# Feed-forward of latents and context: twelve of 22 pairs of up tiles as seven block products, two weight sums by accumulating transfers

## The chip, the core and the metric

The kernel runs on one core of one Trainium2 chip. The metric is device time in microseconds (us); lower is better. One run gives 1257.7 us as the median of three (1257.22 to 1257.75).

## What is computed

A gated-linear-attention block with its feed-forward, then a second block of two layers over 256 latent tokens and 256 context tokens, width 1024, all in float32. The change lies in the feed-forward of the second block's first layer, which both token sets pass through:

```python
def swiglu_ffn(h, w_in, w_out):
    a, g = jnp.split(h @ w_in, 2, axis=-1)
    return (jax.nn.silu(a) * g) @ w_out
# second_block, layer i:
    h = h + g2_l * swiglu_ffn(ada_norm(h, norm_ffn[i], sh2_l, sc2_l), ffn_w_in[i], ffn_w_out[i])
    if ctx_out:      # true for layer 0 only
        hc = hc + g2_c * swiglu_ffn(ada_norm(hc, norm_ffn[i], sh2_c, sc2_c), ffn_w_in[i], ffn_w_out[i])
```

`ffn_w_in` is 1024 x 5632 (the `a` half, then the gate half), `ffn_w_out` 2816 x 1024.

## The kernel before, in words

**Float32 as three products.** Every large matrix product is done in the type fp32r. Each operand is held as a rounded part `h` and a remainder `l`, and `mm3` (L192 to L195) issues three matmuls: h·h, l·h, h·l. Activations are split when they are made, weights when they arrive.

**Weights as a stream.** All weights stand in memory as units of 128 x 1024 floats (512 KB), in the order of use (`UNITS`). `w_load` (L147) brings a unit into one of five `raw` buffers through the SP queue; `w_split` (L161) writes its `wh` on ACT (L178, a cast) and its `wl` on DVE (L179, a subtraction) into two of twelve `w` buffers. `wnext` hands the next unit to the code and asks for loads and splits a few units ahead (`cap`, 3).

**The feed-forward of layer 0.** The hidden width 2816 is 22 feature tiles of 128. For a feature tile f there is a *pair of up tiles*: one unit for `a`, one for the gate, each 8 blocks of 128 x 128 over the input width. `ffn_up` (L1122) multiplies each of the pair's units with the 512 tokens of `fT` (latents and context side by side): 2 units x 8 blocks x 3 matmuls, each with 512 columns, so 48 matmuls. `ffn_act` (L1109) applies Silu on ACT, multiplies on DVE and splits the result. The first two pairs are done by `ffn_up_first` (L1132), context first, in matmuls of 256 columns.

The 22 pairs run in two parts of 11. After each part `ffn_down0` (L1149) multiplies the part's features with `ffn_w_out`, for each half of the output columns: in the first part for all four token tiles at once, in the second for the two context tiles and then for the two latent tiles. `gated` (L1078) scales the sum and adds it to the residual, two DVE instructions for each token tile and half. In the last half of the latents, `to_T` (transposes on PE, L232) for the context of the next layer is called after the third weight unit.

**Other work in the same stretch.** `ada_jobs` streams the modulation weights: 512 KB for a step into one of two `a` buffers (L304), then one or two DVE reductions of 128 x 1024 (L324). `ada_run` advances it at fixed places of the code: two steps after each pair, one after each unit of `ffn_down0`.

**Order.** Except in stretches marked as ordered by hand, the order of instructions on each engine is laid down when the program is built. A planner takes, for each engine, instructions whose operands its own time estimates call ready, the earlier in the code the sooner. On the chip each engine then runs its list strictly in order: one that waits for an operand holds all behind it. On the GpSimd (POOL) queue, as on SP's, the same holds for transfers.

**PSUM.** Eight banks of 128 x 512 floats. A regular pair uses two; `ffn_down0` with four tiles uses four. An engine that reads a bank and a matmul that writes the same bank follow each other in the code's order, even where they touch different columns.

## Time and profile before

| | |
|---|---|
| time, median of 3 runs | 1257.7 us |
| the profiled execution's own time | 1256.72 us |
| its span, first to last instruction | 1254.9 us |
| granted TensorE clock | 0.999 |
| PE busy | 1244.0 us (99%) |
| DVE busy | 919.9 us (73%) |
| ACT busy | 688.2 us (55%) |
| POOL busy | 78.7 us (6%) |
| the feed-forward of layer 0 | from about 565 to 944 us of the span |

The profiled execution is 1 us under the median. A matmul's listed duration includes its passage through the array, so consecutive matmuls overlap in the list; what one costs is read from the distance between starts. The same holds in a smaller measure for DVE and ACT.

### The profile page before, as it was taken

Reading aid. Unit: us, or ns where it says so; the run is one execution under the profiler, and the core shown is the slowest. Engines: PE = TensorE matmul, PEld = TensorE weight load, DVE = VectorE, ACT = ScalarE, POOL = GpSimd, SP = SyncE. Lnnn points to the kernel's source line nnn. Section 1 sums busy time; section 2 is a strip of 40 time slices with the busy share of each in tenths; the row PEclk is TensorE's granted clock in tenths of the full one; section 3 lists DMA queues with packets and bytes.
Section 4 is the critical chain, followed back from the end, with each engine's and each line's share of the span. In section 5 each row is a group of like instructions: output and inputs, shape, how many; then the busy total and the mean of one; then the engine's idle time right before and its main releaser. Section 6 shows DMA issues by size and latency. Waiting matters only on the chain.

```text
span 1254.9 us, 18667 instructions
## 1 busy us (share of the span) xinstructions
PE 1244.0 (99%) x6872; PEld 1043.2 (83%) x6872; DVE 919.9 (73%) x1638; ACT 688.2 (55%) x1344; POOL 78.7 (6%) x137
## 2 busy tenths in 40 slices
PE   9999999999999999999999999999999999999997
PEld 8888889898888777789888888887888777999997
DVE  6959888697989887777877767633667988655555
ACT  8575655666549888655232222323456897544443
POOL 1010000030100000001000000000003220000000
PEclk9999999999999999999999999999999999999999
DMA  8647687787673333463656877633662324656650
GB/s 304 189 151 237 192 289 268 271 277 246 198 249 111 105 110 118 160 197 118 213 177 206 259 266 249 205 100 102 197 204 76 113 84 131 219 187 185 186 185 34
DMA packets 68507, 231.22 MB, mean 184 GB/s; under 512 B 8048, under 2 KB 8736, under 8 KB 68416
## 3 DMA queue, kind: packets, MB, share of 16 engines
q1 hardware_dynamic: 68128, 229.68, 57.0%
q8 instruction: 54, 0.88, 0.3%
q10 hardware_dynamic: 288, 0.35, 0.1%
q14 instruction: 37, 0.30, 0.1%
HBM read 228.93 MB, written 1.07 MB: 183 GB/s over the span
## 4 chain that ended last, share of the span: by engine, by line
PE 95%; ACT 2%; DVE 1%; issue 1%; DMA 0%; POOL 0%; SPq 0%; POOLq 0%; ACTq 0%
PE b L193 28%; PE b L194 28%; PE b L195 28%; PE b L1000 2%; PE b L1469 1%; PE b L981 1%; PE b L232 1%; PE b L1455 1%; PE b L562 1%; PE b L962 1%; PE b L963 1%; PE b L951 1%; PE b L1436 1%; DVE wl L179 0%; DMA t<-in_xt_dram 0%
## 5 line engine op out<-in xcount | busy, mean ns | idle before, releaser
L178 ACT CAST wh<-raw 128x1024 fp32r<-128x1024 f32 (+1 forms) x308 | 320.7, 1045 | 392.8 <-PE b L194 292.4
L179 DVE TENSOR_TENSOR wl<-raw,wh 128x1024 fp32r<-128x1024 f32 (+1 forms) x308 | 372.5, 1216 | 154.9 <-ACT wh L178 151.9
L193 PE MATMUL b<-t,wh 128*128 128x256 f32 (+1 forms) x1120 | 365.7, 327 | 0.0
L194 PE MATMUL b<-t,wl 128*128 128x256 f32 (+1 forms) x1120 | 365.6, 327 | 0.0
L195 PE MATMUL b<-t,wh 128*128 128x256 f32 (+1 forms) x1120 | 365.3, 327 | 0.0
L193 PE MATMUL b<-wh,t 128*128 128x512 f32 (+1 forms) x748 | 299.2, 402 | 1.2 <-ACT t L250 0.6
L194 PE MATMUL b<-wh,t 128*128 128x512 f32 (+1 forms) x748 | 294.8, 394 | 0.0
L195 PE MATMUL b<-wl,t 128*128 128x512 f32 (+1 forms) x748 | 294.7, 394 | 0.0
L193 PEld LDWEIGHTS b<-t,wh 128*128 128x128 f32 x1120 | 210.7, 188 | 22.2
L194 PEld LDWEIGHTS b<-t,wl 128*128 128x128 f32 x1120 | 210.8, 188 | 21.9
L195 PEld LDWEIGHTS b<-t,wh 128*128 128x128 f32 x1120 | 210.5, 188 | 20.4 <-DVE t L251 0.2
L195 PEld LDWEIGHTS b<-wl,t 128*128 128x128 f32 x748 | 140.4, 188 | 34.2
L193 PEld LDWEIGHTS b<-wh,t 128*128 128x128 f32 x748 | 140.4, 188 | 32.2 <-ACT t L250 1.0
L194 PEld LDWEIGHTS b<-wh,t 128*128 128x128 f32 x748 | 140.8, 188 | 30.1 <-DVE t L251 0.5
L324 DVE CUSTOM_DVE_ANT_0 a<-a,crow 128x1024 f32<-128x1024 f32 x96 | 117.6, 1233 | 28.8 <-DMA a<-in_ada_dram 28.3
L324 DVE CUSTOM_DVE_ANT_0 t<-a,crow 128x1024 bf16<-128x1024 f32 x64 | 78.5, 1237 | 7.3 <-DMA a<-in_ada_dram 7.1
L1112 DVE TENSOR_TENSOR t<-b,t 128x512 f32<-128x512 f32 (+1 forms) x42 | 23.7, 564 | 59.4 <-PE b L195 52.2
L205 POOL TENSOR_TENSOR c<-c,mhalf 128x1 f32<-128x1 f32 x21 | 14.2, 676 | 539.0 <-DVE c L204 538.9
L339 POOL TENSOR_TENSOR mod<-mod,bcol 128x8 f32<-128x8 f32 x20 | 13.4, 671 | 475.1 <-DVE mod L324 472.7
L1118 ACT CAST t<-t 128x512 fp32r<-128x512 f32 (+1 forms) x42 | 21.7, 516 | 28.6 <-DVE t L1112 28.6
L212 ACT ACTIVATE t<-t 128x512 f32<-128x512 f32 x40 | 24.8, 624 | 10.8 <-DVE t L1081 6.4
L1445 ACT ACTIVATE t<-b,c,c 128x512 f32<-128x512 f32 x32 | 26.0, 812 | 3.5 <-POOL c L1443 3.5
(244 smaller groups left out, 1212.6 us busy)
## 6 DMA issues: line engine op xcount, KB each, us to landing
raw<-in_wst_dram SPq DMA_DIRECT2D x310, 512.0 KB, 4.4
a<-in_ada_dram SPq DMA_DIRECT2D x96, 512.0 KB, 4.4
t<-in_rpb_dram SPq DMA_DIRECT2D x16, 256.0 KB, 4.5
t<-row SPq DMA_DIRECT2D x12, 256.0 KB, 5.1
t<-in_ctx_dram SPq DMA_DIRECT2D x8, 256.0 KB, 5.6
t<-in_xt_dram SPq DMA_DIRECT2D x4, 256.0 KB, 5.8
t<-in_x_dram SPq DMA_DIRECT2D x4, 256.0 KB, 6.5
crow<-in_cvec_dram SPq DMA_DIRECT2D x2, 512.0 KB
```

Of the source, the lines that this page charges most:

```text
L178: A.copy(out=h[:, :n], in_=raw[:, :n])
L179: V.tensor_tensor(out=l[:, :n], in0=raw[:, :n], in1=h[:, :n], op=ALU.subtract)
L193: T.matmul(o, lhsT=lh, rhs=rh, start=first, stop=False)
L194: T.matmul(o, lhsT=ll, rhs=rh, start=False, stop=False)
L195: T.matmul(o, lhsT=lh, rhs=rl, start=False, stop=last)
L205: G.tensor_tensor(out=ms[:, 3:4], in0=ms[:, 2:3], in1=mhalf[:, 0:1], op=ALU.pow)
L212: A.activation(out=junk[hf], in_=halves[hf], func=AF.Square, scale=1.0 / 32.0, accum_out=ms[:, hf:hf + 1])
L324: V.tensor_tensor_reduce(out=raw if ci == n_c - 1 else t2([D], BF16), in0=raw, in1=crow[ci], scale=1.0, scalar=0.0, op0=ALU.mult, op1=ALU.add,
L1000: T.matmul(po[e * 64:(e + 1) * 64, cols_], lhsT=v, rhs=probs[(head, "l" if lat_q else "c")][:, c, :], start=(c == 0), stop=(c == n_c - 1))
L1112: V.tensor_tensor(out=a, in0=pg_[:, :n], in1=a, op=ALU.mult)
L1118: A.copy(out=h, in_=a)
L1445: A.activation(out=pl, in_=sl, func=AF.Exp, scale=r, bias=mx[:, 1:2], accum_out=mx[:, 2:3])
```

## The change

For feature tiles 10 to 21 the pair of up tiles is done as a 2 x 2 by 2 x 2 block product in seven block products in place of eight. The blocks of the weights are `a` and gate, each by the lower and upper 512 of the input width; the blocks of the data are latents and context, by the same halves. Each block product is 4 blocks x 3 matmuls of 256 columns.

- `ffn_up7` issues the seven products. Four of them (the first, third, fifth and seventh) accumulate one after the other in the same bank `r`, which is copied out between them: the third continues the sum that the first left, and so on. The second and fourth go to the two halves of bank `r23`, the sixth to `r4`. In all 84 matmuls of 256 columns, three ACT copies, two Silus, seven DVE operations of 256 columns, and the split of the result.
- The four sums of weight blocks are made for each pair as it arrives. `w_load` takes a third `raw` buffer `z`: half a unit of `a` is loaded into it by SP, and two transfers from the POOL queue add a half of the gate unit onto `z` and the other half of the gate unit onto the gate's own buffer. `pair_sums`, a generator with four steps, does the other two sums on DVE and the splits: three of 1024 columns, one of 512. The steps are called from within the pair before (`run(conv, 2)` at its start, one each after its second and fourth product).
- The four sums of data blocks are made once, by `token_sums`, during the second half of the first `ffn_down0`. For them `to_T` keeps the unsplit transposed data in `fX`.
- The latents and the context stand in separate tiles `fL` and `fC`, so that regular pairs (`ffn_up`) issue 96 matmuls of 256 columns in place of 48 of 512.
- Three parts of 8, 8 and 6 pairs replace two of 11. `ada_run` is not called in the seven-product pairs, and twice for each unit of `ffn_down0` with four tiles. `load_gates(0, 5)` is called after each part. The last `to_T` is called after the second unit.

```diff
@@ -26,7 +26,8 @@
 NFT = FH // P
-HALF = NFT // 2
+PARTS = ((0, 8), (8, 16), (16, 22))
+F_SEVEN = 10
@@ -58,11 +59,11 @@
     u += o + o
-    for part in range(2):
-        for f in range(part * HALF, (part + 1) * HALF):
+    for lo, hi in PARTS:
+        for f in range(lo, hi):
             u += [("f", "ffn_in0", P * f), ("f", "ffn_in0", FH + P * f)]
-        dn = [("h", "ffn_out0", part * HALF + f, 512 * h) for h in range(2) for f in range(0, HALF, 2)]
-        u += dn if part == 0 else dn + dn
+        dn = [("h", "ffn_out0", f, 512 * h) for h in range(2) for f in range(lo, hi, 2)]
+        u += dn if hi < NFT else dn + dn
     kv = [("h", "gqa_qkv", 2 * k, D) for k in range(4)]
@@ -149,6 +150,14 @@
             raws[wpos[0]] = raw
+            if seven(UNITS[wpos[0]]) and UNITS[wpos[0]][2] >= FH:
+                x, y = [wst[SLOT[UNITS[wpos[0] + n]]] for n in (-1, 0)]
+                z = sb.tile([P, 1024], F32, tag="raw", bufs=5, name=nm("raw"))
+                nc.sync.dma_start(out=z[:, 0:512], in_=x[:, 0:512])
+                G.dma_start(out=z[:, 0:512], in_=y[:, 0:512], accum_op=ALU.add)
+                G.dma_start(out=raw[:, 0:512], in_=y[:, 512:1024], accum_op=ALU.add)
+                raws[wpos[0]] = (raw, z)
             wpos[0] += 1
@@ -162,7 +171,7 @@
             raw = raws.pop(i)
-            n = 512 if UNITS[i][0] == "h" and UNITS[i][1] == "ffn_out0" and (UNITS[i][2] % HALF) == HALF - 1 else 1024
+            n = 1024
             h = sb.tile([P, 1024], F32R, tag="w", bufs=NW, name=nm("wh"))
@@ -178,21 +187,25 @@
+    def seven(u):
+        return u[1] == "ffn_in0" and u[2] % FH >= P * F_SEVEN
     def wnext(kind):
         w_split(i + 1)
-        while wpos[1] < len(UNITS) and wpos[1] - wpos[2] + 1 < cap[0]:
+        while wpos[1] < len(UNITS) and wpos[1] - wpos[2] + 1 < cap[0] and not seven(UNITS[wpos[1]]):
             w_load(wpos[1] + 4)
-    def mm3(o, lh, ll, rh, rl, first, last):
-        T.matmul(o, lhsT=lh, rhs=rh, start=first, stop=False)
-        T.matmul(o, lhsT=ll, rhs=rh, start=False, stop=False)
-        T.matmul(o, lhsT=lh, rhs=rl, start=False, stop=last)
+    def mm3(o, lh, ll, rh, rl, first, last, onto=False):
+        T.matmul(o, lhsT=lh, rhs=rh, start=first, stop=False, skip_group_check=onto)
+        T.matmul(o, lhsT=ll, rhs=rh, start=False, stop=False, skip_group_check=onto)
+        T.matmul(o, lhsT=lh, rhs=rl, start=False, stop=last, skip_group_check=onto)
@@ -223,7 +236,7 @@
-    def to_T_steps(xns, dst, t0, scale=None, bias=None):
+    def to_T_steps(xns, dst, t0, scale=None, bias=None, keep=None):
@@ -240,7 +253,7 @@
             else:
-                r = t2([n])
+                r = t2([n]) if keep is None else keep[k]
                 if k % 2:
@@ -1098,11 +1111,12 @@
-    fT = new_T2()
+    fL, fC = new_T(), new_T()
+    fX = [t2([2, S]) for _ in range(KD)]
     o_half(1, 2, hc, 1)
     o_half(0, 0, lat, 0)
-    o_half(1, 0, lat, 0, lambda: to_T(xn, fT, S, mod(0, 1, 4), mod(0, 1, 3)))
+    o_half(1, 0, lat, 0, lambda: to_T(xn, fC, 0, mod(0, 1, 4), mod(0, 1, 3), [z[:, 1, :] for z in fX]))
     xn = [normed(t) for t in lat]
@@ -1119,43 +1133,152 @@
-    def ffn_up(L, src, n):
+    def ffn_up(L, src, n, conv=iter(())):
         ps_ = []
             o = bank()
-            for k in range(KD):
-                mm_f(o[:, :n], u, src, k, 0, n, k == 0, k == KD - 1)
+            for t, X in enumerate(src):
+                for k in range(KD):
+                    mm_f(o[:, t * S:(t + 1) * S], u, X, k, 0, S, k == 0, k == KD - 1)
+            run(conv, 2)
             ps_.append(o)
-    def ffn_up_first(src):
+    def ffn_up_first():
             for k in range(KD):
-                mm_f(os_[-1][:, S:N2], us[-1], src, k, S, S, k == 0, k == KD - 1)
-        to_T(xn, src, 0, mod(0, 0, 4), mod(0, 0, 3))
+                mm_f(os_[-1][:, S:N2], us[-1], fC, k, 0, S, k == 0, k == KD - 1)
+        to_T(xn, fL, 0, mod(0, 0, 4), mod(0, 0, 3), [z[:, 0, :] for z in fX])
         z = []
             for k in range(KD):
-                mm_f(os_[n][:, 0:S], us[n], src, k, 0, S, k == 0, k == KD - 1)
+                mm_f(os_[n][:, 0:S], us[n], fL, k, 0, S, k == 0, k == KD - 1)
             if n % 2:
-    def ffn_down0(hf, uu, tiles, between=None):
+    sT = {}
+    def token_sums(j):
+        lo, hi, q = fX[j], fX[j + KD // 2], t2([2, S])
+        V.tensor_tensor(out=q[:, 1, :], in0=hi[:, 1, :], in1=lo[:, 1, :], op=ALU.subtract)
+        V.scalar_tensor_tensor(out=q[:, 0, :], in0=q[:, 1, :], scalar=-1.0, in1=lo[:, 0, :], op0=ALU.mult,
+                               op1=ALU.subtract)
+        V.tensor_tensor(out=lo[:, 1, :], in0=lo[:, 0, :], in1=lo[:, 1, :], op=ALU.subtract)
+        V.scalar_tensor_tensor(out=lo[:, 0, :], in0=q[:, 0, :], scalar=-1.0, in1=hi[:, 0, :], op0=ALU.mult,
+                               op1=ALU.subtract)
+        for z, names in ((q, (2, 1)), (lo, (4, 3))):
+            h, l = t2([2, S], F32R), t2([2, S], F32R)
+            A.copy(out=h, in_=z)
+            V.tensor_tensor(out=l, in0=z, in1=h, op=ALU.subtract)
+            for i, name in enumerate(names):
+                sT[(name, j)] = (h[:, i, :], l[:, i, :])
+    def pair_sums(f, got):
+        i = wpos[1]
+        assert UNITS[i] == ("f", "ffn_in0", P * f)
+        w_load(i + 4)
+        x, (y, z) = raws.pop(i), raws.pop(i + 1)
+        wpos[1] += 2
+        a, b = slice(0, 512), slice(512, 1024)
+        def parts(r):
+            h = sb.tile([P, 1024], F32R, tag="w", bufs=NW, name=nm("wh"))
+            l = sb.tile([P, 1024], F32R, tag="w", bufs=NW, name=nm("wl"))
+            A.copy(out=h, in_=r)
+            V.tensor_tensor(out=l, in0=r, in1=h, op=ALU.subtract)
+            got.append((h, l))
+        parts(x)
+        yield
+        V.tensor_tensor(out=z[:, b], in0=z[:, a], in1=y[:, b], op=ALU.add)
+        parts(z)
+        yield
+        parts(y)
+        yield
+        V.tensor_tensor(out=x[:, a], in0=z[:, b], in1=x[:, b], op=ALU.add)
+        hl = sb.tile([P, 1024], F32R, tag="w", bufs=NW, name=nm("w"))
+        A.copy(out=hl[:, a], in_=x[:, a])
+        V.tensor_tensor(out=hl[:, b], in0=x[:, a], in1=hl[:, a], op=ALU.subtract)
+        got.append((hl[:, a], hl[:, b]))
+        yield
+    def splits(n):
+        for _ in range(n):
+            w_split(wpos[1] + 1)
+            yield
+    def ffn_up7(got, conv):
+        wpos[2] += 2
+        r, r23, r4 = bank(), bank(), bank()
+        c1, c2 = t2([2, S]), t2([2, S])
+        H = KD // 2
+        def prod(o, n, c, X, first=True):
+            h, l = got[n]
+            for j in range(H):
+                k = slice(c + j * P, c + (j + 1) * P)
+                mm3(o, h[:, k], l[:, k], *X(j), first and j == 0, j == H - 1, not first)
+        run(conv, 2)
+        prod(r[:, 0:S], 0, 0, lambda j: fL[j])
+        A.copy(out=c1[:, 0, :], in_=r[:, 0:S])
+        prod(r23[:, 0:S], 0, 512, lambda j: fL[H + j])
+        got[0] = None
+        V.tensor_tensor(out=c1[:, 0, :], in0=r23[:, 0:S], in1=c1[:, 0, :], op=ALU.add)
+        run(conv)
+        prod(r[:, 0:S], 1, 512, lambda j: sT[(2, j)], False)
+        A.copy(out=c1[:, 1, :], in_=r[:, 0:S])
+        A.activation(out=c1[:, 0, :], in_=c1[:, 0, :], func=AF.Silu)
+        prod(r23[:, S:N2], 2, 512, lambda j: sT[(4, j)])
+        run(conv)
+        prod(r[:, 0:S], 1, 0, lambda j: sT[(1, j)], False)
+        got[1] = None
+        A.copy(out=c2[:, 0, :], in_=r[:, 0:S])
+        V.tensor_tensor(out=c2[:, 1, :], in0=c1[:, 1, :], in1=c2[:, 0, :], op=ALU.subtract)
+        V.tensor_tensor(out=c2[:, 0, :], in0=r23[:, S:N2], in1=c2[:, 0, :], op=ALU.add)
+        V.tensor_tensor(out=c2[:, 0, :], in0=c2[:, 0, :], in1=c1[:, 0, :], op=ALU.mult)
+        prod(r4[:, 0:S], 3, 0, lambda j: fC[H + j])
+        V.tensor_tensor(out=c2[:, 1, :], in0=r4[:, 0:S], in1=c2[:, 1, :], op=ALU.add)
+        prod(r[:, 0:S], 2, 0, lambda j: sT[(3, j)], False)
+        V.tensor_tensor(out=c2[:, 1, :], in0=r[:, 0:S], in1=c2[:, 1, :], op=ALU.add)
+        A.activation(out=c2[:, 1, :], in_=c2[:, 1, :], func=AF.Silu)
+        V.tensor_tensor(out=c2[:, 1, :], in0=r[:, 0:S], in1=c2[:, 1, :], op=ALU.mult)
+        a = c2.rearrange("p t s -> p (t s)")
+        h, l = t2([N2], F32R), t2([N2], F32R)
+        A.activation(out=h, in_=a, func=AF.Copy, scale=-1.0)
+        V.scalar_tensor_tensor(out=l, in0=a, scalar=-1.0, in1=h, op0=ALU.mult, op1=ALU.subtract)
+        return h, l
+    def ffn_down0(hf, uu, tiles, between=None, conv=None):
         ac = {t: bank() for t in tiles}
-        for f2 in range(0, HALF, 2):
+        for f2 in range(0, len(uu), 2):
             u = wnext(("h", "ffn_out0"))
-            for j in range(min(2, HALF - f2)):
+            for j in range(2):
                 f = f2 + j
                 for t in tiles:
-                    mm_h(ac[t], u, j, uu[f], t, f == 0, f == HALF - 1)
-            ada_run(adaC)
-            if f2 == 4 and between is not None:
+                    mm_h(ac[t], u, j, uu[f], t, f == 0, f == len(uu) - 1)
+            ada_run(adaC, 2 if len(tiles) == 4 else 1)
+            if hf == 1 and len(sT) < 16:
+                token_sums(f2 // 2)
+            if conv is not None and f2 >= len(uu) - 4:
+                run(conv, 2)
+            if f2 == 2 and between is not None:
                 between()
@@ -1178,18 +1301,29 @@
-    for part in range(2):
+    got = []
+    for lo, hi in PARTS:
         uu = []
-        for f in range(HALF):
-            if part == 0 and f < 2:
-                uu += ffn_up_first(fT) if f == 0 else []
+        for f in range(lo, hi):
+            nxt = []
+            if f + 1 < hi:
+                conv = pair_sums(f + 1, nxt) if f + 1 >= F_SEVEN else iter(())
             else:
-                uu.append(ffn_up(0, fT, N2))
-            ada_run(adaC, 2)
-        if part == 0:
-            load_gates(0, 5)
-            for hf in range(2):
-                ffn_down0(hf, uu, (2, 3, 0, 1))
+                conv = splits(2) if f >= F_SEVEN else iter(())
+            if f < 2:
+                uu += ffn_up_first() if f == 0 else []
+            elif f < F_SEVEN:
+                uu.append(ffn_up(0, (fL, fC), N2, conv))
+            else:
+                uu.append(ffn_up7(got, conv))
+            got = nxt
+            if f < F_SEVEN:
+                ada_run(adaC, 2)
+        load_gates(0, 5)
+        if hi < NFT:
+            ffn_down0(0, uu, (2, 3, 0, 1))
+            got = []
+            ffn_down0(1, uu, (2, 3, 0, 1), None, pair_sums(hi, got) if hi >= F_SEVEN else None)
         else:
@@ -1646,8 +1780,7 @@
             k, c = s[2], s[3]
-            n = 1 if s[1] == "ffn_out0" and k % HALF == HALF - 1 else 2
-            a[i].reshape(P, 2, 512)[:, :n] = m[k * P:(k + n) * P, c:c + 512].reshape(n, P, 512).transpose(1, 0, 2)
+            a[i].reshape(P, 2, 512)[...] = m[k * P:(k + 2) * P, c:c + 512].reshape(2, P, 512).transpose(1, 0, 2)
     return a
```

More of the change, by code (lines that the diff above doesn't have):

```diff
@@ L1524, in net @@
     tok_T(toks[0], 0, ups)
-    up2 = ffn_up(1, eT, S)
+    up2 = ffn_up(1, (eT,), S)
     tok_T(toks[1], 1, ups)
```

2 lines of the change are left out of this document (1 added, 1 removed).

## The prediction

> **What bounds the kernel now.** I read the page's busy times and its chain first, then a table by stretches of the feed-forward (columns: stretch, its us, busy us and instructions of each engine, granted clock, DMA share, GB/s).
>
> ```profile
> span 1254.9 us, 18667 instructions
> PE 1244.0 (99%) x6872; PEld 1043.2 (83%) x6872; DVE 919.9 (73%) x1638; ACT 688.2 (55%) x1344; POOL 78.7 (6%) x137
> PE 95%; ACT 2%; DVE 1%; issue 1%; DMA 0%; POOL 0%; SPq 0%; POOLq 0%; ACTq 0%
> ...
> 565.00:690.00 125.00, 125.00 (x610) 103.61 (x609) 96.18 (x148) 42.42 (x65) 6.92 (x18) 1.00 0.57 179
> 690.00:752.00 62.00, 62.00 (x268) 49.86 (x267) 44.16 (x68) 12.51 (x13) 1.52 (x3) 1.00 0.80 261
> 752.00:875.00 123.00, 123.00 (x527) 98.84 (x526) 64.24 (x85) 35.15 (x46) 3.35 (x3) 1.00 0.52 166
> ```
>
> PE is busy through all of the first part's pairs (565 to 690), its down products (690 to 752) and the second part's pairs (752 to 875), at clock 1.00. So a matmul taken out here shortens the kernel, as long as nothing new makes PE wait. What a matmul costs is read from starts: the first and last of 66 consecutive matmuls of 512 columns, then of 38 consecutive ones of 256 columns, from the next layer's up products.
>
> ```profile
> 584.74 0.39 PE L194 MATMUL b<-t,wl 128*128 128x512 f32 x1
> ...
> 599.97 0.40 PE L193 MATMUL b<-t,wh 128*128 128x512 f32 x1
> ...
> 1099.76 0.28 PE L194 MATMUL b<-t,wl 128*128 128x256 f32 x1
> ...
> 1104.10 0.28 PE L195 MATMUL b<-t,wh 128*128 128x256 f32 x1
> ```
>
> 15.23/65 = 0.2343 us, and 4.34/37 = 0.1173 us: half the columns cost half the time. The weight load in front of each does not show.
>
> **The change part by part. PE first.** A regular pair is 48 x 0.2343 = 11.25 us. A seven-product pair is 84 x 0.1173 = 9.85 us. Twelve pairs save 12 x 1.39 = 16.7 us. The regular pairs 2 to 9 go to 96 x 0.1173 = 11.26 us: 8 x 0.01 = +0.1 us. The down products keep their count.
>
> The Trainium skill, "TensorE: Matmul & The Clock Gate", section "Back-to-back issue gap", gives a sustained spacing of 81 ns at 128 columns and 131 ns at 512, which would make a narrow matmul dear for its columns. The rows above differ from it in both size and ratio, and the measurement decides.
>
> **What must stay hidden beside PE: DVE and ACT in a seven-product pair.** Their cost too is read from starts. The DVE rows (from two stretches) and the ACT rows:
>
> ```profile
> 600.40 1.22 DVE L179 TENSOR_TENSOR wl<-raw,wh 128x1024 fp32r<-128x1024 f32 x1
> 601.54 1.22 DVE L324 CUSTOM_DVE_ANT_0 a<-a,crow 128x1024 f32<-128x1024 f32 x1
> ...
> 607.85 0.69 DVE L1119 TENSOR_TENSOR t<-t,t 128x512 fp32r<-128x512 f32 x1
> 608.45 1.22 DVE L324 CUSTOM_DVE_ANT_0 t<-a,crow 128x1024 bf16<-128x1024 f32 x1
> ...
> 250.32 0.43 DVE L808 TENSOR_TENSOR t<-t,t 128x256 fp32r<-128x256 f32 x1
> 250.67 1.22 DVE L324 CUSTOM_DVE_ANT_0 t<-a,crow 128x1024 bf16<-128x1024 f32 x1
> ...
> 578.11 1.04 ACT L178 CAST wh<-raw 128x1024 fp32r<-128x1024 f32 x1
> 579.05 0.62 ACT L1118 CAST t<-t 128x512 fp32r<-128x512 f32 x1
> ...
> L1462 ACT COPY t<-b x64: 359/388/513, 985.4 to 1052.4; 128x256 f32<-128x256 f32 x64
> L1111 ACT ACTIVATE t<-b 128x256 f32<-128x256 f32 x20 | 7.6, 379 | 1.6 <-PE b L195 1.6
> ```
>
> DVE takes 1.14 us for 1024 columns, 0.60 for 512, 0.35 for 256. For a pair: three subtractions of 1024 (3.42), two sums, the remainder of the fourth and that of the result, all of 512 (4 x 0.60 = 2.40), and seven operations of 256 (2.45): 8.3 us of 9.85, or 84%. ACT: three casts of 1024 (0.94 each by starts), two of 512 (0.62), three copies and two Silus of 256 (0.39 and 0.38): 6.0 us, 60%. Both fit, if in time.
>
> **The handovers.** Here is what the change adds to PE's path. The third product writes the bank `r` that ACT must first copy; so do the fifth and seventh; the fourth writes bank `r23`, which DVE reads after the second. At each only one product of 12 x 0.1173 = 1.41 us lies between, so from the start of the last matmul before to the first matmul behind there is 1.41 + 0.12 = 1.53 us. How soon a reader follows:
>
> ```profile
> 616.60 0.39 PE L195 MATMUL b<-t,wh 128*128 128x512 f32 x1
> ...
> 617.10 0.69 DVE L1112 TENSOR_TENSOR t<-b,t 128x512 f32<-128x512 f32 x1 [2.47 <-PE b L195]
> ```
>
> 0.50 us after that start, DVE is there. With 0.4 us for its own work, some 0.6 us of slack remains. An instruction that is under way can take it. One of DVE's 1.14 us, met at random, has more than 0.6 left in 47% of cases, 0.27 too much on average: at 84% busy 0.84 x 0.47 x 0.27 = 0.11 us. A second one queued ahead adds 1.14; I let that happen in a quarter of the cases, 0.29. On ACT, 0.60 x 0.36 x 0.17 = 0.04 us at each of three. Together 0.5 us for a pair, an estimate from these rows. The ends are 0 (every handover free) and 4 x 1.7 = 6.8 (every one behind two long instructions); the value lies near the low end because three of the four handovers are ACT's. 12 x 0.5 = +6.0 us.
>
> **The adding transfers.** No transfer from POOL's queue stands in this trace. The nearest rows are SP's:
>
> ```profile
> raw<-in_wst_dram SPq DMA_DIRECT2D x7, 512.0 KB, 3.7
> ...
> t<-in_rpb_dram SPq DMA_DIRECT2D x16, 256.0 KB, 4.5
> ...
> out_dram<-t SPq DMA_DIRECT2D x3, 256.0 KB, 2.0
> ...
> t<-in_gk_up_dram SPq DMA_DIRECT2D x2, 32.0 KB, 6.6
> ```
>
> So a load of 256 KB is 2.0 to 4.5 us, an adding one 2.0 to 6.6 behind it (not under 2.0, as it too moves 256 KB and reads its target besides). `z` needs both in turn: 4.0 to 11.1 us; I take 8. The buffer for the `z` of pair n+2 is that of pair n+1's gate unit, free once it is split, and that waits for two `w` buffers (of twelve, seven hold pair n's parts), free after pair n's second product: 2.8 + 0.94 + 1.14, so about 5 us into pair n. `z` is there 3 us into pair n+1 (1 us before its start to 6 us into it). PE needs its parts at the third product of pair n+2, another 9 us on, so the transfers' length costs nothing by itself. What a late one can do is hold DVE's list at the sum on `z` with the urgent bank readers behind it: that is the main rival. Extra bytes: 1.75 MB for a pair in 9.85 us, 178 GB/s, under the 261 of the second stretch.
>
> **The rest, all beside PE.** One part more is eight `gated` more, 16 x 0.60 = 9.6 us of DVE, while the next pair uses the four banks that are free. `token_sums` makes DVE's time for a down unit 1.14 + 2 x 1.2 + 2.6 = 6.1 us against PE's 24 x 0.2343 = 5.6, 2 us over four units; splits made ahead cover it, since ACT's splits stood 122.3 us waiting for PE to free `w` buffers. The waits between 565 and 860 us, the `a` reductions after 722 us, and the end of the last context down product:
>
> ```profile
> ACT wh L178 <- PE b L194: 122.3, 34, 5.0
> ...
> DVE a L324 <- DMA a<-in_ada_dram: 28.3, 19, 4.0
> ...
> L324 DVE CUSTOM_DVE_ANT_0 a<-a,crow x26: 1218/1225/1227, 722.1 to 802.2; 128x1024 f32<-128x1024 f32 x26
> ...
> 900.32 0.69 DVE L1080 TENSOR_TENSOR t<-b,t 128x512 f32<-128x512 f32 x1 [1.42 <-PE b L195]
> ...
> 908.01 0.88 DVE L219 TENSOR_SCALAR t<-t,c 128x512 f32<-128x512 f32 x2 [0.66 <-POOL c L205]
> ...
> 924.62 1.69 PE L232 MATMUL b<-cm,t 128*128 128x128 f32 x14
> ```
>
> Eight weight units fewer take 8 loads off SP. Eight more 256 KB gate rows (`load_gates`) go on it; they are needed a down product later. The last context norm has less time: it was done 8.6 us after the context's last product (900.3 to 908.9), and PE came to the transposes at 924.6. Now it comes to them after 36 + 24 matmuls of 0.2343, 14 us, still behind the norm. Nothing for any of these; if the last cover fails, 1 to 3 us.
>
> **Sum.** -16.7 + 0.1 + 6.0 = -10.6 us: span 1254.9 to 1244.3, that execution 1256.7 to 1246.1. The median is 1.0 above the profiled execution: 1257.7 - 10.6 = 1247.1 us.
>
> **Rivals.** *Full saving*: every handover meets its 0.6 us. For it: list order lets bank readers come early. 1257.7 - 16.6 = 1241.1.
>
> *Late sums (slower)*: the list order is laid down with estimated transfer times, and DVE stands at the sum on `z` while the second product's reader queues behind. For it: DVE already waited 19 times, 28.3 us in all, up to 4.0 us, for `a` transfers. Against it: no wait for a `raw` load is among the long ones of that stretch. Ten pairs are exposed (each part's first is loaded long before). A lateness of L costs (L - 0.6) x 10: at the mean 1.5 us, 9 us, still faster; it decides from 2.3 us on; at 4.0 us, 34 - 16.6 = +17, so 1275. The Trainium skill speaks for this one: "SBUF — State Buffer", section "A bandwidth-pool intuition that's wrong (but worth ruling out)", has a POOL-issued transfer wait for its descriptors behind a DVE copy, 620 ns becoming about 3100; the same page exempts DVE's two-input operations, which fill these pairs, and no run here shows either. With those 2.5 us as L the formula would give +2 us, an estimate.
>
> *DVE full (no change)*: the 26 `a` reductions that ran from 722 to 802 us, far ahead of the place where the code has them, are pulled into the first seven-product pairs, which have 1.5 us free each, and so each handover meets a full engine. Against it: at most six or seven pairs are hit. PE loses the saved 1.39 us in each: 1256 to 1258.
>
> *Narrow matmuls dearer*: the seven products change nothing if 256 columns cost more than 11.25/84 = 0.134 us. The 38 matmuls above stand against it. By the skill's two spacings, interpolated to 98 ns, the ratio would be 0.75 for half the columns: 12 x 3.4 + 8 x 5.5 = +85 us, 1343.
>
> **How the numbers follow.** Forecast (1243 to 1252) 0.47; full saving 0.22; DVE full 0.10; late sums beyond 2.3 us 0.19; narrow matmuls 0.02. About 0.2% (2.5 us) is what a measurement of this kernel can tell from no change. Faster is the first two: 0.69; same 0.10; slower 0.21. The range runs from the full saving, 1240.5, to late sums of about 2.7 us, 1262, and leaves out the longer ones and the last rival, some 0.15 together.
>
> **What would show it.** Right: 256-column starts 0.117 us apart in the seven-product pairs, a pair in 9.9 to 10.6 us, PE's idle time there under 12 us, released by ACT copies or the DVE sum of `r23`. Wrong: DVE idle at the sum on `z` with POOL's transfer as releaser; a pair at 11 us or more; DVE over 95% busy in the first six.

## The result and the profile after

The changed kernel takes 1311.9 us (1308.8 to 1319.2) against 1257.7 us: ratio 1.044, 95% interval 1.040 to 1.048. It is 54 us slower, where 10.6 us less was forecast.

The page of the changed kernel, the lines that answer to those shown of before (span, busy times, the chain by engine), with the clock in 40 slices (9 is 90% or more); the last line is the clock of before:

```profile
span 1309.4 us, 20652 instructions
PE 1256.4 (96%) x7688; PEld 1091.3 (83%) x7688; DVE 989.6 (76%) x1790; ACT 718.5 (55%) x1416; POOL 100.5 (8%) x161
...
PEclk9999999999999999999999788998999999999999
...
PE 28%; DMA 3%; DVE 3%; ACT 2%; issue 1%; POOL 0%; POOLq 0%; ACTq 0%; DVEq 0%; SPq 0%
...
PEclk9999999999999999999999999999999999999999
```

The feed-forward by stretches (stretch, its us, busy us and instructions of PE, PEld, DVE, ACT, POOL, then granted clock, DMA share, GB/s):

```profile
565.00:700.00 135.00, 135.00 (x954) 125.81 (x954) 102.19 (x158) 38.95 (x56) 11.06 (x22) 1.00 0.60 186
700.00:800.00 100.00, 77.70 (x554) 75.39 (x554) 84.75 (x148) 33.17 (x55) 9.82 (x12) 0.85 0.72 214
800.00:900.00 100.00, 91.46 (x543) 79.89 (x541) 67.24 (x104) 35.29 (x54) 8.60 (x11) 0.97 0.59 172
900.00:1000.00 100.00, 89.89 (x502) 77.57 (x502) 65.58 (x108) 46.40 (x84) 5.17 (x7) 0.93 0.51 160
```

Up to 700 us PE is as full as before, at clock 1.00. From there PE idles 22, 8.5 and 10 us of each hundred, and, what no row of before had, its clock falls: 0.15 + 0.03 + 0.07 of 100 us is 25 us of clock, or 50 us at half clock if it falls to half. DVE is not the bound over these hundreds (85, 67 and 66%).

PE's time between its starts can be split for the feed-forward (from 565 us to the start of its last transpose). A spacing within 5% of the nominal one (0.2343, 0.1173, and 0.109 us for the 128-column ones) counts whole as "full speed". Of a longer one the nominal part counts as full speed, and what is over it as "slow" if it is up to about as much again, as "idle" if it is more. Before it is 380.1 + 0.9 + 0.1 us; after, 365.8 + 21.0 + 48.0. So the change did take 14.3 us off the matmuls, and 68.0 us of stalls and slow matmuls were put on. The same split is given for the experiments below.

Who made PE and DVE wait (waits between 700 and 1000 us: us in total, times, longest):

```profile
PE b L206 <- ACT t L1240: 14.1, 4, 4.2
PE b L206 <- DVE t L1093: 8.6, 1, 8.6
PE b L206 <- ACT w L1216: 3.6, 2, 2.6
PE b L206 <- ACT t L1246: 3.1, 1, 3.1
...
DVE raw L1209 <- DMA raw<-in_wst_dram: 40.4, 10, 6.1
```

L1240 and L1246 are ACT's copies of `r`, L1216 the cast of the fourth half-width unit: what PE waits for directly. In the turn shown next, L1240 stands in ACT's list behind a cast that waits for DVE (786.70), and DVE stands at L1209, the sum on `z`, ten times for 40.4 us in all. One turn of that loop, from the timelines of the engines:

```profile
769.90 0.69 DVE L1209 TENSOR_TENSOR raw<-raw,raw 128x512 f32<-128x512 f32 x1 [4.19 <-DMA raw<-in_wst_dram]
...
773.19 1.22 DVE L1204 TENSOR_TENSOR wl<-raw,wh 128x1024 fp32r<-128x1024 f32 x1
...
774.48 0.33 SPq L157 DMA_DIRECT2D raw<-in_wst_dram  x1
775.90 1.59 SPq L151 DMA_DIRECT2D raw<-in_wst_dram  x2
...
777.99 0.87 POOL L158 DMA_DIRECT2D raw<-in_wst_dram  x1 [9.89 <-ACT wh L1203]
...
784.75 0.28 PE L208 MATMUL b<-t,wh 128*128 128x256 f32 x1
...
785.93 0.69 DVE L1209 TENSOR_TENSOR raw<-raw,raw 128x512 f32<-128x512 f32 x1 [3.44 <-DMA raw<-in_wst_dram]
...
786.70 1.04 ACT L1203 CAST wh<-raw 128x1024 fp32r<-128x1024 f32 x1 [3.76 <-DVE raw L1209]
...
788.18 0.35 ACT L1240 COPY t<-b 128x256 f32<-128x256 f32 x1
...
788.59 0.58 PE L206 MATMUL b<-t,wh 128*128 128x256 f32 x1 [3.56 <-ACT t L1240]
788.97 0.42 PE L207 MATMUL b<-t,wl 128*128 128x256 f32 x1
789.18 0.41 PE L208 MATMUL b<-t,wh 128*128 128x256 f32 x1
```

`z` is summed at 769.90, and split at 773.19. As that split ends (774.41) SP, which has waited for it, issues the load of the next `z` (774.48): the next `z` goes into the buffer of this one. The next two units follow (775.90, 777.16) as the last readers of the pair's other two buffers end (775.88, 777.14). 3.5 us after the load's issue POOL issues the adding transfer (777.99), and that lands 7.9 us later, when DVE goes on (785.93). 16.0 us from sum to sum, for a pair of 9.9 us of matmuls. In the five pairs from 728.64 to 808.37 us, 84 starts take 14.5 to 16.8 us; in four of the last part (868.69 to 918.20) they take 10.1 to 15.4, so there the loop is not always the limit. PE, without its copy of `r`, stands from 784.75 to 788.59, and its next starts are 0.21 us apart instead of 0.117: the clock has been halved. SP's waits for such a split between 700 and 960 us (eight of the twelve loads), and the landing times of the transfers over the whole kernel (SP's load of `z`, the transfer onto `z`; from issue, least, median, most):

```profile
SPq L157 <- DVE wl L1204: 30.8, 8, 9.1
...
L157 SPq DMA_DIRECT2D raw<-in_wst_dram x12: 327/328/333, 681.3 to 910.2; - x12
...
DMA to landing us min/median/max: 2.6/3.0/4.5
...
L158 POOL DMA_DIRECT2D raw<-in_wst_dram x12: 865/865/880, 687.7 to 913.7; - x12
...
DMA to landing us min/median/max: 4.1/5.6/7.9
```

The longest single stall has another cause. The timeline around it:

```profile
703.48 0.42 DVE L1178 TENSOR_TENSOR t<-t,t 128x256 f32<-128x256 f32 x1
...
727.21 0.68 DVE L1187 TENSOR_TENSOR t<-t,t 128x512 fp32r<-128x512 f32 x1
727.81 1.28 DVE L1093 TENSOR_TENSOR t<-b,t 128x512 f32<-128x512 f32 x2
...
728.64 0.55 PE L206 MATMUL b<-t,wh 128*128 128x256 f32 x1 [8.61 <-DVE t L1093]
```

The data sums (L1178 to L1187) were listed inside the first down product, but ran only from 703 to 728 us, with `a` reductions between them; `gated` (L1093) came behind them in DVE's list, so the four banks that it reads stayed taken for 8.6 us of PE's time. Why they ran so late isn't shown.

A third, smaller: the chain of waits has `t<-row`, the gate rows that are now loaded once more in each part, twice as the last thing waited for. The last line is from the list of DVE's waits.

```profile
833.66 6.48 DMA t<-row
...
961.13 6.83 DMA t<-row
967.99 1.29 DVE t L1093 x2
...
974.76 0.88 DVE t L232 x2
...
977.30 0.77 PE b L245 x5
...
DVE t L1093 <- DMA t<-row: 1.6, 1, 1.6
```

The 6.5 and 6.8 us run from SP's issue to the landing; they aren't waits. DVE stood for a row only once, 1.6 us, in front of the last `gated` (967.99), and so before the norm (L232) ahead of the closing transposes (L245). At the first, up to 839.56, it stood at L1209 for the adding transfer.

### The profile page after: what moved, and what is told of

Same layout as the page of the kernel before. It is cut to its first block, busy times and chain, and to the rows that moved or that the text cites. A ratio compares the mean times of both kernels' runs of the same rounds, so it can differ in the third digit from the quotient of the medians.

```text
span 1309.4 us, 20652 instructions
## 1 busy us (share of the span) xinstructions
PE 1256.4 (96%) x7688; PEld 1091.3 (83%) x7688; DVE 989.6 (76%) x1790; ACT 718.5 (55%) x1416; POOL 100.5 (8%) x161
## 5 line engine op out<-in xcount | busy, mean ns | idle before, releaser
L187 ACT CAST wh<-raw 128x1024 fp32r<-128x1024 f32 x276 | 289.2, 1053 | 271.2 <-PE b L207 217.3
L188 DVE TENSOR_TENSOR wl<-raw,wh 128x1024 fp32r<-128x1024 f32 x276 | 336.1, 1227 | 130.4 <-ACT wh L187 128.6
L206 PE MATMUL b<-t,wh 128*128 128x256 f32 (+1 forms) x1344 | 400.4, 299 | 29.2 <-ACT t L1240 14.1
L207 PE MATMUL b<-t,wl 128*128 128x256 f32 (+1 forms) x1344 | 397.7, 296 | 0.5 <-DVE wl L1204 0.5
L208 PE MATMUL b<-t,wh 128*128 128x256 f32 (+1 forms) x1344 | 396.5, 296 | 0.0
L206 PEld LDWEIGHTS b<-t,wh 128*128 128x128 f32 x1344 | 259.6, 193 | 41.7 <-ACT t L1240 14.9
L207 PEld LDWEIGHTS b<-t,wl 128*128 128x128 f32 x1344 | 260.3, 194 | 8.3 <-DVE wl L1204 0.7
L208 PEld LDWEIGHTS b<-t,wh 128*128 128x128 f32 x1344 | 259.3, 193 | 5.8 <-DVE t L264 0.2
L1203 ACT CAST wh<-raw 128x1024 fp32r<-128x1024 f32 x36 | 37.6, 1046 | 57.5 <-DVE raw L1209 25.2
L1204 DVE TENSOR_TENSOR wl<-raw,wh 128x1024 fp32r<-128x1024 f32 x36 | 43.8, 1220 | 11.7 <-ACT wh L1203 4.3
L352 POOL TENSOR_TENSOR mod<-mod,bcol 128x8 f32<-128x8 f32 x20 | 13.1, 654 | 382.0 <-DVE mod L337 379.6
L1209 DVE TENSOR_TENSOR raw<-raw,raw 128x512 f32<-128x512 f32 x12 | 8.3, 691 | 44.5 <-DMA raw<-in_wst_dram 44.5
L1126 DVE TENSOR_TENSOR t<-b,t 128x256 f32<-128x256 f32 (+1 forms) x30 | 15.4, 513 | 29.4 <-PE b L208 25.7
```

The lines of the kernel that those rows point to most:

```text
L187: A.copy(out=h[:, :n], in_=raw[:, :n])
L188: V.tensor_tensor(out=l[:, :n], in0=raw[:, :n], in1=h[:, :n], op=ALU.subtract)
L206: T.matmul(o, lhsT=lh, rhs=rh, start=first, stop=False, skip_group_check=onto)
L207: T.matmul(o, lhsT=ll, rhs=rh, start=False, stop=False, skip_group_check=onto)
L208: T.matmul(o, lhsT=lh, rhs=rl, start=False, stop=last, skip_group_check=onto)
L352: G.tensor_tensor(out=m, in0=m, in1=bcol[:, L, v, :], op=ALU.add)
```

## The experiments

### Is it the adding transfers, and which part of them?

`e1_dve_sums`: all four sums on DVE.

```
-   nc.sync.dma_start(out=z[:, 0:512], in_=x[:, 0:512])
-   G.dma_start(out=z[:, 0:512], in_=y[:, 0:512], accum_op=ALU.add)
-   G.dma_start(out=raw[:, 0:512], in_=y[:, 512:1024], accum_op=ALU.add)
...
+   V.tensor_tensor(out=z[:, a], in0=x[:, a], in1=y[:, a], op=ALU.add)
+   V.tensor_tensor(out=y[:, a], in0=y[:, a], in1=y[:, b], op=ALU.add)
```

> All four sums of weight blocks on DVE; no load of z and no transfer from the POOL queue; the rest as changed. Theory A (the adding transfers close a loop: z's buffer free, load, add, sum, split of the gate unit, next buffer free; 16 us for a pair): PE's idle time in the seven-product pairs, about 25 us, and most of the half-clock spells behind it go; time 1311.9 - 25 - 12 = about 1275 us, although DVE has 1.2 us more for each pair. Rival B (DVE is simply full in these pairs, with the reductions of the modulation weights pulled in): more DVE work makes it worse, 1312 to 1330 us.

`e2_no_adding`: the two `G.dma_start` lines left out, so that two of the four sums are missing; `z` is still loaded.

> The two adding transfers are left out and nothing takes their place, so two of the four sums of weights are missing; z is still loaded by SP. Theory A: the loop loses its 5.5 to 8 us for the add, a pair falls from 16 to about 10 us, PE idle in the pairs under 5 us, time 1311.9 - 25 - 12 = about 1275 us. Rival B (DVE full): DVE's work is unchanged, so 1305 to 1312 us.

1272.1 us (ratio 1.011, 1.008 to 1.014) and 1267.2 us (one run). 40 of the 54 us go with the adding transfers (split for e1: 365.3 + 8.8 slow + 22.3 idle). In e2 the load of `z` still waits for its buffer (SP waits for a split, L1202 there, seven times for 29.3 us in all) and does no such harm: it is the transfer behind it that makes the loop too long.

`e11_raw6`: one raw buffer more.

```
-   raw = sb.tile([P, 1024], F32, tag="raw", bufs=5, ...)      NT2 = 58
+   raw = sb.tile([P, 1024], F32, tag="raw", bufs=6, ...)      NT2 = 56
```

> The changed kernel with a sixth raw weight buffer (and two of 58 buffers of t fewer, which pays for its room); the adding transfers stay. Theory (the loop: z is loaded only when a buffer of the pair before comes free at z's own sum, and the adding transfer then lands 4 to 8 us after its issue): with one spare buffer more z can be loaded and added to ahead, the pair falls from 16 us to about 11, DVE's wait at the z sum goes from 44.5 us to under 10, and the time to about 1275 to 1285. Rival (the adding transfers are slow by themselves, or DVE's order holds the loop): the wait stays above 30 us and the time at 1300 or more.

1296.4 us (one run): the time lies between the two theories, the wait above the rival's 30. DVE's wait for the sum on `z`, and the transfer onto it, over the whole kernel:

```profile
DVE raw L1209 <- DMA raw<-in_wst_dram: 31.3, 8, 8.5
...
L158 POOL DMA_DIRECT2D raw<-in_wst_dram x12: 865/950/1162, 679.6 to 890.3; - x12
...
DMA to landing us min/median/max: 4.7/6.5/10.1
```

The wait was 44.5 us in the changed kernel and is 31.3. The buffer was a part; but the load and the transfer one after the other take about as long as a pair's 9.9 us or longer by themselves (in one turn load at 768.55, transfer at 771.60, landed at 778.55: 10.0 us; over the twelve turns 8.9 to 14.9), and the transfers land later still. A lone sixth buffer doesn't hide that.

`e17_one_add`: only the transfer onto `y`, whose buffer is loaded a pair ahead, is kept; `z` is made of it on DVE.

```
-   nc.sync.dma_start(out=z[:, 0:512], in_=x[:, 0:512])
-   G.dma_start(out=z[:, 0:512], in_=y[:, 0:512], accum_op=ALU.add)
...
-   V.tensor_tensor(out=z[:, b], in0=z[:, a], in1=y[:, b], op=ALU.add)
+   V.tensor_tensor(out=z[:, b], in0=x[:, a], in1=y[:, a], op=ALU.add)
+   V.tensor_tensor(out=z[:, a], in0=z[:, b], in1=y[:, b], op=ALU.subtract)
```

> The changed kernel with one adding transfer of two: y's first half is still added to by a transfer, onto a buffer that is loaded a pair ahead; the sums of z are two operations on DVE (x + y + y', then less y'), and z is neither loaded nor added to by a transfer. Three instead of two sums per pair on DVE (0.68 us each). Theory (only the chain of z's load and the transfer onto z, which starts when the pair before gives its buffers back, is too long): as good as with all four sums on DVE or a little better, 1262 to 1275, and DVE waits for raw less than 10 us in all. Rival (any adding transfer beside this traffic lands too late): DVE waits over 25 us for the buffer of y, 1285 or more.

1272.2 us (one run), as with no transfer at all, and no wait of DVE for `raw` is left among its waits. This transfer is hardly quicker:

```profile
L157 POOL DMA_DIRECT2D raw<-in_wst_dram x12: 856/868/1098, 680.7 to 873.1; - x12
...
DMA to landing us min/median/max: 3.9/5.0/7.5
```

So an adding transfer of 4 to 8 us does no visible harm here where its target has been there for a pair, and twelve of them cost 40 us where each follows a load that itself waits for the consumer. The theory of the loop holds, with the transfer onto `z` as its longest piece.

### What are the other 14 us?

`e3_gates_once`: `if lo == 0:` ahead of `load_gates(0, 5)`.

> The gate rows are loaded once, after the first part, as in the kernel before; the rest as changed. If the repeated rows cost what the trace shows (DVE's gated waits for rows 6.5 us at 834 and 6.8 us at 961, PE idle 2.5 us at 839 and 5.5 us from 974 to 984), 8 us of idle time and some 3 us of half clock go: 1301 us. Rival: these waits only take the place of others (late sums, hand-over at the end), 1309 to 1313 us.

`e4_sums_after`: the loop over `token_sums` moved behind the `gated` steps of the first down product.

> The sums of the data blocks are called after the gated additions of the first down product, not before them; the rest as changed. Theory C (the data sums find no free t buffers until that product has ended, run late on DVE, and hold the gated additions behind them, so that the four banks stay taken and PE stands 8.8 us at 720): 8.8 us of idle time, 2 us right behind it and some 6 us of half clock go, 1295 us. Rival: the same work only moves into the first seven-product pairs, which need these sums, 1308 to 1320 us.

1306.0 and 1304.8 us: some 6 and 7 us each, less than each theory gave (the first of which took the 6.5 and 6.8 us above for waits). Each is one run, and the four of the changed kernel lie between 1308.8 and 1319.2, so the size of these gains isn't shown. In e4 PE's largest stalls are no longer on L1093; it waits 9.9 us on the copies L1246 and 9.9 on the casts L1216 instead: the sums now stand among the work of the pairs, and so does most of the stall (split 364.6 + 18.9 + 45.0).

`e5_no_seven`: `F_SEVEN = 22` and no data sums: everything else of the change, with eight products throughout.

> All 22 pairs in eight block products, and no sums of data; the three parts, the separate latents and context, the places of the modulation steps, the repeated gate rows and the earlier transposes stay as changed. If the rest of the change is free, as the prediction put it, 1257 to 1259 us. If the repeated gate rows and the earlier transposes cost what the trace of the changed kernel shows (2.5 + 5.5 us idle and some half clock), 1265 to 1269 us. 1275 us or more would mean that the seven products are not the main loss.

1261.6 us (one run), between the two: the frame alone costs about 4 us. Its split is 383.5 + 1.0 + 1.6 against 380.1 + 0.9 + 0.1 before, so this isn't mainly stalls. A stretch of the kernel before with PE full and nothing but 512-column matmuls:

```profile
650.00:690.00 40.00, 40.00 (x173) 32.16 (x172) 29.83 (x44) 10.75 (x14) 2.23 (x2) 1.00 0.61 194
```

and one of e5 with nothing but 256-column ones:

```profile
730.00:780.00 50.00, 50.00 (x424) 50.00 (x423) 36.75 (x55) 13.91 (x19) 0.40 (x2) 1.00 0.82 273
```

From the first start to the last, over 170 and 420 spacings (the rows count a few more, which reach in over the edges), that is 0.2341 and 0.1187 us. Two narrow matmuls take 0.2373, 0.0032 us more than a wide one, and e5 splits 20 x 48 = 960: 3.1 us, of the 3.4 by which the first part of the split grew.

`e6_all`: e1, e3 and e4 together.

> Three edits together: all four sums of weights on DVE, gate rows loaded once, sums of data after the gated additions. By theory A, C and the rows each adding its part to the 1272 us of the DVE sums alone: gate rows -6 (measured alone -5.9), data sums -7 (alone -7.1): 1259 us. If they only hide one another, 1268 to 1272 us.

1270.4 us (1.010, 1.007 to 1.013), only 2 us under e1, with two runs each: not clear of their spread. With the transfers gone, neither edit was worth its 6 us. The trace shows that the stall of the data sums has moved: PE idles 5.4 and 2.8 us in front of the first seven-product pairs (722.5 and 733.5 us), where e1 has 2.7 and 6.1 (719.0 and 726.1).

### From there to what the change can give

`e9_from12`: e6, the closing transposes of context one down unit later (`f2 == 4`), and `F_SEVEN = 12`.

> The three edits, the transposes for the next layer again after the third unit, and seven-product pairs from feature tile 12 on (ten in place of twelve), which gives DVE two regular pairs, 22.5 us, more to finish the data sums. Saving of the products 10 x 1.39 = 13.9 us. If DVE's backlog at the start of the first seven-product pairs (9 us of idle time in the run with DVE sums) and the closing transposes (6 us) were what was left, 1246 to 1250 us, faster than before; if the pairs lose at every handover as the prediction assumed (0.5 us each), 1250 to 1255; if DVE stays full, 1258 or more.

`e10_ada1`: e6 with the later transposes and one ada step instead of two beside each down unit, `F_SEVEN = 10`.

> The three edits, the late transposes, twelve seven-product pairs, and one modulation step for each down unit in place of two. If the modulation reductions crowd DVE at 697 to 735 us (eight of 1.14 us among the data sums in the run with DVE sums), PE's idle time there falls from 9 us to under 4 and the time is 1244 to 1250 us; if the planner pulls the same reductions forward anyway, the time is that of the three edits together, about 1255 to 1259.

1265.0 and 1264.3 us (1.006 and 1.005): both missed the values hoped for. In e10 the closing still stops PE for 3.7 us at the transposes, and the clock is 0.94 between 900 and 955 us.

`e12_last8`: e10 with `PARTS = ((0, 8), (8, 14), (14, 22))`.

> All four weight sums on DVE, gate rows loaded once, data sums behind the gated steps, later transposes, one ada step per down unit (as e10_ada1), and parts of 8, 6 and 8 units in place of 8, 8 and 6. Theory (what is left at the end is the closing: the last gated steps, the norm and the transposes of context have too little matmul work left beside them): two more units in the last part cover it, PE's gaps of 3.7 us and the half clock behind them at the end go, 1257 to 1260. Rival (the closing gap is the chain from the last gated to the transposes and moves along, as the norm starts no earlier against the last down product): 1263 to 1266.

`e13_from14`: e12 with `F_SEVEN = 14`.

> As e12_last8, with only the last eight pairs (from 14 on, all of the last part) as seven products. Saving of 8 x 1.39 = 11 us on what the same kernel without seven-product pairs takes (1261.6 in e5_no_seven), less a handover of 0.5 to 0.8 us for each of eight pairs (4 to 6.4): 1255 to 1257 by the theory that ada steps and data sums beside the first six pairs are the rest of what is lost, and near 1250 if moving the last part also mends the closing. Rival (seven-product pairs are bound by DVE's own 9 to 10 us of sums and splits wherever they stand): 1261 to 1265, no better than with twelve.

1258.2 us for e12 (1.0008, 0.9998 to 1.0019): the two units more in the last part do cover the closing, which is most of these 6 us, and the clock between 900 and 950 us is back at 1.00. 1260.1 for e13 (1.002, 1.001 to 1.003): fewer pairs, away from the ada steps, are not better; the first pair behind the down product stands 2.6 us for DVE there. In e12 the stalls left are the handovers:

```profile
PE b L202 <- ACT t L1238: 3.9, 7, 0.7
...
834.00:872.00 38.00, 35.23 (x279) 33.18 (x277) 38.00 (x68) 19.73 (x34) 0.00 (x0) 1.00 0.51 171
```

L1238 is the copy of `r` (L1240 in the changed kernel): 0.4 to 0.9 us a time between PE's starts, behind a cast of 1.05 us. The second row is a stretch of some three pairs: DVE 100% busy, PE idle for 2.8 us of 38, and 84 starts in 11.6 us. A regular pair takes 11.25, so these pairs save nothing.

`e14_best`: e13 with the next two edits; `e15_best12`: e12 with them. Latents and context are kept side by side in one buffer, so that eight-product pairs keep their 512 columns; and the fourth and sixth products of a pair change banks, so that the fourth no longer writes the bank that DVE is reading.

```
-   fL, fC = new_T(), new_T()
+   fT = new_T2()        # fL, fC are its halves
...
-   prod(r23[:, S:N2], 2, 512, ...)        prod(r4[:, 0:S], 3, 0, ...)
+   prod(r4[:, 0:S], 2, 512, ...)          prod(r23[:, S:N2], 3, 0, ...)
```

> As e13_from14, with two more edits: one buffer holds latents and context side by side, so that the eight-product pairs keep matmuls of 512 columns, and the fourth and sixth products of a seven-product pair change banks, so that the fourth no longer waits for DVE's sum of the third. Theory (the narrow matmuls cost 0.0032 us per matmul split, 24 x 2 x 12 = 576 of them, 1.8 us; the wait before the fourth product 0.3 to 0.4 us for seven pairs and 2.6 for the first): 4 to 6 us less than 1257 to 1260, so 1251 to 1255. Rival (DVE or ACT, in order, are late by as much at the next product; the stall only moves): 1256 to 1259, no better than before.

> As e12_last8 with the same two edits, twelve pairs of seven products. Theory as for e14_best: 24 x 2 x 8 = 384 matmuls no longer split (1.2 us), 0.3 to 0.4 us in each of twelve pairs (4): 1252 to 1254. Rival (DVE with the ada steps in the first pairs is the bound, and it has no less to do): 1256 to 1258.

e14 1259.9 us (1.002, 1.001 to 1.003), no better than e13, as its rival had it: there PE waits for L1238 (1.3 us), L1200 (1.9) and L1241 (1.4) instead. e15 1252.2 us, ratio 0.995 (0.9935 to 0.9965): the first version faster than before, by half a percent. The two edits were made together; by the split (below, for e15_again) the wide matmuls give 2.4 us of the gain on e12, fewer stalls and slow matmuls 4.9.

`e18_one_add12`: e15 with e17's single transfer. `e15_again`: the kernel of e15 once more.

> e15_best12 with one of the four sums, onto y, by an adding transfer (three on DVE). Theory (a transfer onto a buffer that is loaded a pair ahead is hidden, and DVE, 96% busy between 700 and 900 us, has 0.68 us less per pair): 0 to 3 us less than e15_best12's 1252, so 1249 to 1252. Rival (the transfer of y holds y's buffer and its split, and y's part is late in the first pairs): 1254 to 1260.

> The same kernel as e15_best12, on the chip of e18_one_add12: 1251 to 1253, faster than before by 0.4 to 0.5%.

e15 again 1251.0 us (0.995, 0.994 to 0.997). e18 1255.4 (0.9986, 0.9976 to 0.9995): still a little faster than before, but 4.4 us behind e15, though DVE has a sum of 512 columns, 0.60 us, less to do in each pair. The transfer lands in 4.0 to 6.5 us there. Between 700 and 800 us PE is busy for 95.0 us (97.0 in e15_again) at clock 0.98, with DVE at 92%, so DVE isn't fuller. Why wasn't settled. An adding transfer buys nothing in this stage. The feed-forward of e15_again, and PE's waits in it:

```profile
700.00:800.00 100.00, 97.00 (x590) 85.28 (x589) 97.17 (x165) 42.64 (x65) 1.17 (x2) 1.00 0.53 174
800.00:900.00 100.00, 99.66 (x731) 93.26 (x731) 95.56 (x157) 52.69 (x85) 0.58 (x1) 1.00 0.58 192
...
PE b L203 <- DVE wl L1200: 1.7, 1, 1.7
PE b L202 <- ACT t L1238: 0.7, 2, 0.6
```

DVE is 96 to 97% busy, and PE loses 3.3 us in 200, most of them in front of the first seven-product pair. The splits of the stages side by side, in us:

| kernel | full speed | slow | idle | sum | time |
|---|---|---|---|---|---|
| before | 380.1 | 0.9 | 0.1 | 381.1 | 1257.7 |
| after | 365.8 | 21.0 | 48.0 | 434.9 | 1311.9 |
| e1_dve_sums | 365.3 | 8.8 | 22.3 | 396.4 | 1272.1 |
| e5_no_seven | 383.5 | 1.0 | 1.6 | 386.1 | 1261.6 |
| e10_ada1 | 365.7 | 7.3 | 16.4 | 389.4 | 1264.3 |
| e12_last8 | 366.2 | 4.3 | 11.9 | 382.3 | 1258.2 |
| e15_again | 363.8 | 3.3 | 8.0 | 375.1 | 1251.0 |

The first column holds the saving, 14 to 16 us in every kernel with twelve seven-product pairs; nearly all that they differ by stands in the other two.

## Why the prediction was wrong

**Right, or nearly.** A 256-column start: 0.118 us in the seven-product pairs of e15_again and 0.1187 in e5, against 0.1173 taken; 14.3 us saved, against 16.7 less 0.1. The narrow matmuls of the regular pairs were put at +0.1 us; by e5's 0.0032 us each it is 8 x 48 x 0.0032 = 1.2. The place of the handovers was right, their size too low: 0.5 us a pair predicted; in e12 0.4 to 0.9 us at the copy of `r` and about 0.3 at the sum of `r23`, and 11.9/12 = 1.0 us of idle time for each pair in all. Where most of what was costed at nothing has been made to cost little, in e15, -5.5 to -6.0 us are left of the -10.6. Two of the three signs of being wrong were there: DVE idle at the sum on `z` with POOL's transfer as releaser, and pairs of 11 us or more.

**The step that failed first: "so the transfers' length costs nothing by itself".** `z`'s load and transfer were put at 4.0 to 11.1 us with 8 taken; the turn shown takes 11.5 from SP's issue to DVE's sum, a little over the upper end. The larger error is in the start: the buffer for the next `z` was held to be that of a gate unit, free about 5 us into a pair, from splits that were reckoned as independent of `z`. In the trace the load goes out as the split of the `z` before it ends, which stands behind that `z`'s own sum in DVE's list. With that, a lateness is handed on; each `z` waits for the one before, and the pair takes the length of the loop, 16 us in the turn shown. The rival *late sums* named the place and its releaser, and e1, e2 and e17 bear it out; but its formula took a lateness as a fixed number with a chance of its own. At the measured mean, 44.5/11 = 4.0 us, it gives (4.0 - 0.6) x 10 - 16.6 = +17 us. The rest of the 54 was not in it.

**"Nothing for any of these."** The data sums were held to be covered by splits made ahead, 2 us over four units. What they took was a place in DVE's list: `gated` queued behind them and kept four PSUM banks (8.6 us). "They are needed a down product later" was said of the gate rows; in the trace the last `gated` waits 1.6 us for them, and the closing norm, which the prediction saw done in time, was late. "If the last cover fails, 1 to 3 us" was too little: most of 6 us, with the slow matmuls behind the stalls, by e12 against e10. What each of these is worth alone isn't shown: taken away alone (e3, e4) each gave 6 to 7 us in one run, both on top of e1 only 2.

**What the sum lacked altogether: the clock.** Before, PE never stopped and all rows showed 1.00; the prediction counted a stall as its length. In the changed kernel slow matmuls took 21.0 us beyond their nominal time against 0.9, so its 48 us of stalls cost 20 us more, about 0.4 us for each.

**DVE.** *DVE full* had ada steps drawn into the first six pairs, and the saved 1.39 us lost in each. It wasn't the main loss: in the changed kernel DVE is 85, 67 and 66% busy. But with the transfers' sums on DVE it comes true in part: `a` reductions stand among the pairs (seven of them in e12's 834 to 872 us), DVE is 100% busy there, and a pair takes 11.6 us. In e15_again, with DVE at 96 to 97% and all four sums on it, pairs after the first (13.1) take 10.0 to 11.3 us. So over 95%, which was to be the sign of failure, doesn't settle it. That it depends on whether the reader of a bank stands behind a long instruction fits e12's stalls at L1238; e14, where the same two edits gave nothing, leaves it open.

## What to carry to other kernels

Before giving work to a transfer, ask what frees its target: if that hangs on the result of the transfer before, its latency is the period of a loop and not something that runs beside the matmuls, and a spare buffer helps only if the chain is shorter than the work it is to hide behind. An engine whose list is in order makes everything behind a late step late, so of each added instruction ask whose bank or buffer is freed by the next one in that list. And on a matrix engine that was never idle, a stall of some microseconds can cost its length and a slow spell after it; the covers "at nothing" are to be priced with that.

## What the runs showed of the hardware

After PE had stood still for 3.8 us (784.75 to 788.59) it went on at 0.21 us per 256-column matmul until 794.29. The first row is from that spell, with a granted clock of 0.50; the second from the end of the longest stall (8.9 us between starts, to 728.64) and what follows it:

```profile
788.60:793.20 4.60, 4.60 (x21) 4.60 (x22) 4.03 (x8) 2.52 (x5) 0.00 (x0) 0.50 0.62 186
...
724.00:735.00 11.00, 5.31 (x25) 4.97 (x25) 11.00 (x21) 3.13 (x6) 0.88 (x1) 0.60 0.57 154
```

Stalls of 0.3 to 0.9 us in every pair (e12) leave it at 1.00. The Trainium skill, "TensorE: Matmul & The Clock Gate", section "Part 1: The HAM clock gate", has the array drop to half clock after one idle window of about 3.4 us and come back after one busy window. Its 256 columns at 1.2 GHz, by estimate 0.213 us, are the spacing seen here, and the stalls of 3.3 us and more in the changed kernel's feed-forward were all followed by such a spell. Shorter ones don't all fit: by the rule a stall of 2.3 us should leave the clock alone, and one in e10 (838.94 us) was followed by such a spell, while one of 2.6 us in e13 (802.88) was not. Two stalls of 0.7 and 1.9 us with a single matmul between them were followed by one in e15_best12 (726 to 729 us) and not in e15_again, which is the same kernel.

An adding transfer of 256 KB lands 3.8 to 10.1 us after POOL issues it, with medians of 4.3 to 6.5 in the kernels that have it, and takes POOL 0.87 us in the changed one; a plain load of 256 KB from SP beside it 2.6 to 4.5. The Trainium skill, "DMA: Bandwidth & Descriptors", section "Anatomy of one DMA — SWDGE (gpsimd) path", fits 2.0 us plus bytes over 436,000 for a transfer from this queue, which would be 2.6 us by estimate; the measured ones, which add and in the changed kernel run beside 160 to 214 GB/s of traffic (the stretches above), are longer in every case.
